# Seven block products for gate and up in all three feed-forwards, with the weight sums formed in DRAM

## The chip, the cores and the metric

The kernel runs on one core of a Trainium2 chip. The metric is the device time of one execution in microseconds (us). Before the change it is 2364.4 us, the median of three runs (2363.6 to 2364.85).

## The reference

Two transformer blocks follow each other, in float32, on 512 tokens of width 1024. The first block puts 16 meta tokens in front, so it works on 528. Cut to its frame:

```python
def first_block(...):                       # h: 528 tokens x 1024
    for l in range(2):
        hn = rmsnorm(h, norm_mix[l])
        h = h + (even_mixer if l == 0 else odd_mixer)(hn, ...)   # sparse attention + retention; stick-breaking attention
        h = h + conv_ffn(rmsnorm(h, norm_ffn[l]), ...)
    return rmsnorm(h, norm_final)[:, 16:528]

def conv_ffn(h, w_up, w_gate, conv_w, conv_b, w_down):           # 1024 -> 2816 -> 1024
    g = causal_conv3(h @ w_gate) + conv_b                        # over tokens, one filter per column
    return (silu(g) * (h @ w_up)) @ w_down

def second_block(x, ...):                                        # x: 512 tokens
    x = x + merge(four_mixers(rms_norm(x, attn_norm))) @ w_merge_out
    h = rms_norm(x, ffn_norm)
    return x + (silu(h @ w_gate) * (h @ w_up)) @ w_down
```

Each block ends its layers with a feed-forward: two `conv_ffn` in the first, one without a convolution in the second. The kernel calls them ffn0, ffn1 and ffn2.

## The kernel before

**Data.** The residual stream lies transposed in SBUF: eight tiles `h0` to `h7`, 128 columns of the model by 528 tokens. Weights lie in DRAM as tiles of 128 x 1024 float32 (512 KB): eight blocks of 128 x 128, one for each 128 rows of the contraction. A feed-forward has 22 tiles of hidden columns, f = 0 to 21, each with one weight tile for gate and one for up.

**A product.** `wtile` loads a weight tile into `w_raw` by a DMA on SP's queue, casts it to `w_hi` (float32r, on ScalarE or VectorE) and forms `w_lo` = `w_raw` - `w_hi` on VectorE. Each of the three names has three buffers. Activations come as the same kind of pair (`xh`, `xl`). `mm3` then makes three matmuls for each block: hi by hi, hi by lo, lo by hi. A plain projection of one weight tile over 528 tokens is two halves of 8 x 3 matmuls with 264 columns each; over 516 tokens they have 258, and over 512 tokens there are 24 matmuls of 512 columns.

**Order.** Every operation goes through the class `Order`, which only records. `flush`, once for each stage, is a list scheduler: it walks through modelled time with a cost for each operation (`cost`) and a delay between engines (`latency`), and issues on each engine the ready operation of lowest priority number. `O.shift -= 500` in `wtile` moves weight loads and their splits ahead by 500 operations. Some copies may go to ScalarE or VectorE, whichever is free first in the model. The chip then runs each engine's queue in that order. All recorded operations stand at one line of the file, L493.

**Stages.** The even mixer takes the span up to about 435 us, ffn0 to 806, the odd mixer to 1112, ffn1 to 1500, the second block's mixer to 1972, ffn2 to the end. Each stage ends with a prefetch of the next stage's first three weight tiles.

**ffn0 and ffn1 (`ffn`).** For each f, `gate_up` projects gate, scales it by the row norm `r`, convolves over tokens on VectorE (`y`), applies silu, projects up, multiplies, and splits the product into `ah`, `al`. Up works on 528 tokens in ffn0 and on 512 in ffn1. `down` takes hidden tiles in three groups, `GROUPS` (8, 8 and 6 tiles): all eight row blocks m of the output of a group come after the first tile of the next group, and `add_h` adds each onto `h`. The last group's row blocks are followed by `Following.add`, which prepares the next stage's `xh`, `xl` and the norm's sum of squares (`acc`).

**ffn2 (`block2_ffn`).** From f = 2 on (`FS`), gate and up are seen as a 2 x 2 block product (two halves of the contraction, two halves of the tokens) and made by `gate_up_fast` with seven half products instead of eight: 7 x 4 x 3 = 84 matmuls of 256 columns. The activations' sums `th`, `tl` are made once at the stage's start. The weights' sums `s13`, `s24` are made for each f in `weights`, on VectorE, by one addition of 1024 columns and two of 512 out of the loaded `r1`, `r2` (their names in the trace are `w_raw` and `s_raw`, since a `Ring` deals out the three `w_` places and two more `s_` places in turn).

**GpSimd** does nothing but its start-up; all DMAs are on SP's queue.

Of the kernel before, what the change touches and what calls it, by code (L numbers as in the profile page):

```python
# [11 lines left out]
F32 = mybir.dt.float32  # L12
# [16 lines left out]
GROUPS = ((0, 8), (8, 16), (16, 22))  # L29
# [160 lines left out]
def prepare(i):  # L190
# [23 lines left out]
    for n, (f0, f1) in enumerate(GROUPS):  # L214
        a[f"w_dn2_{n}"] = pack(i["w_down_2"][0][f0 * P:f1 * P], whole(0, D))
# [152 lines left out]
def latency(a, b):  # L368
    return 2.1 if a == "SP" else LAT.get((a, b), 0.25)
# [12 lines left out]
class Order:  # L382
# [30 lines left out]
    def cost(self, eng, method, out, ins, k):  # L413
# [19 lines left out]
        return 0.1 + n * 2.2e-3  # L433
# [151 lines left out]
def body(ctx: ExitStack, tc, A, out):  # L585
# [18 lines left out]
    class AllBanks:  # L604
# [35 lines left out]
    gg = cst.tile([P, KD], F32, name="gg")  # L640
    gcol = lambda n, k: gains[:, 8 * n + k:8 * n + k + 1]
# [12 lines left out]
    def wtile(name, i, kt=KD):  # L654
# [12 lines left out]
        O.shift += 500  # L667
        return v2(hi, P), v2(lo, P)
# [173 lines left out]
    def even_mixer():  # L842
        with ExitStack() as es:
            P_ = lambda name, **k: O.pool(es, name, **k)
            dr = P_("dr1", bufs=1, space=DRAM)
            ec = P_("ec", bufs=1)
# [268 lines left out]
            for m in range(RF, KD):  # L1115
                add(m)
            prefetch("w_gu0", 0, 1, 2)
            O.flush()

    def ffn(l, n):  # L1120
# [6 lines left out]
        with ExitStack() as es:  # L1127
# [8 lines left out]
            acts = {}  # L1136

            def gate_up(f):
                g = fp.tile([P, gw + 2], F32, name="g")
                V.memset(g[:, 0:2], 0.0)  # L1140
                proj(pall, wtile(f"w_gu{l}", 2 * f), x, times(g[:, 2:], r), grange)
                y = fp.tile([P, uw], F32, name="y", bufs=3)
# [6 lines left out]
                proj(pall, wtile(f"w_gu{l}", 2 * f + 1), xu, times(y, y), urange)  # L1149
                acts[f] = split_new(y, fp, "ah", "al", 10, uw)  # L1150

            def down(gi):
                f0, f1 = GROUPS[gi]
                a = [acts[f][0] for f in range(f0, f1)], [acts[f][1] for f in range(f0, f1)]
                if gi == 2:
                    if l == 0:
                        add = follow(lambda m: gcol(2, m), 0, fp, "y", 3)
                    else:
                        V.tensor_tensor(gg, gains[:, 32:40], gains[:, 40:48], op=ALU.mult)
                        add = follow(lambda m: gg[:, m:m + 1], NM, fp, "y", 3, lambda m: gcol(4, m))  # L1160
                for m in range(KD):
                    proj(pall, wtile(f"w_dn{l}_{gi}", m, f1 - f0), a, add_h(m, u0), urange)
                    if gi == 2:
# [11 lines left out]
    def odd_mixer():  # L1175
# [8 lines left out]
        with ExitStack() as es:  # L1184
            P_ = lambda name, **k: O.pool(es, name, **k)
            op = P_("op", bufs=1)
            x = nxt_[0].x
# [141 lines left out]
            out_proj(1, OSP, KD, follow(lambda m: gcol(3, m), Q0, op, "otmp", 2))  # L1329
            prefetch("w_gu1", 0, 1, 2)  # L1330
# [5 lines left out]
    def block2_mixer():  # L1336
        with ExitStack() as es:
# [5 lines left out]
            unit = lambda name, bufs=1, p=P, dt=F32: wk.tile([p, S], dt, name=name, bufs=bufs)  # L1343

# [377 lines left out]
            for m in range(KD):  # L1722
                proj(pall, wtile("w_mg", m), mgx, add_h(m, NM), ONE)
                add(m)
            prefetch("w_gu2", 0, 1, 2)
            O.flush()

    def block2_ffn():
        with ExitStack() as es:
# [6 lines left out]
            class Ring:  # L1736


                def __init__(self, dt, *places):
                    self.dt, self.places, self.n = dt, places, 0  # L1740

                def tile(self):
                    pl, name, bufs = self.places[self.n % len(self.places)]
                    self.n += 1
                    return pl.tile([P, D], self.dt, name=name, bufs=bufs)

            ring = lambda dt, a, b: Ring(dt, *((wp, a, 3), (fp, b, 2)) * 2, (wp, a, 3))
            raws, his, los = ring(F32, "w_raw", "s_raw"), ring(F32R, "w_hi", "s_hi"), ring(F32R, "w_lo", "s_lo")

            def early(fn):  # L1750
                O.shift -= 500
                v = fn()
                O.shift += 500
                return v

            def halves(raw, hi=None, lo=None):

                n = raw.shape[1]
                hi = his.tile()[:, :n] if hi is None else hi
                lo = los.tile()[:, :n] if lo is None else lo  # L1760
                SC.copy(hi, raw)
                V.tensor_tensor(lo, raw, hi.bitcast(F32), op=ALU.subtract)
                return v2(hi, P), v2(lo, P)

            def load(name, i, n=D):
                raw = raws.tile()[:, :n]
                dma(raw, A[name][i])
                return raw

            ts = []
            for k in range(KD // 2):
                g1, g2 = gcol(6, k), gcol(6, k + 4)
                h1, h2 = hT[k][:, NM:], hT[k + 4][:, NM:]
                tt = v2(raws.tile(), HS)
                th, tl = (fp.tile([P, 4, HS], F32R, name=f"{n}{k}", bufs=1) for n in ("th", "tl"))
                b22 = fp.tile([P, HS], F32, name="sp", bufs=2)
                SC.activation(b22, h2[:, HS:], AF.Copy, scale=g2)
                V.tensor_tensor(tt[:, 0, :], h1[:, :HS], h1[:, HS:], op=ALU.subtract)  # L1780
                SC.activation(tt[:, 0, :], tt[:, 0, :], AF.Copy, scale=g1)
                V.tensor_tensor(tt[:, 1, :], b22, tt[:, 0, :], op=ALU.add)
                V.scalar_tensor_tensor(tt[:, 2, :], h1[:, HS:], g1, b22, op0=ALU.mult, op1=ALU.subtract)
                V.scalar_tensor_tensor(tt[:, 3, :], h2[:, :HS], g2, tt[:, 1, :], op0=ALU.mult, op1=ALU.subtract)
                SC.copy(th, tt)
                V.tensor_tensor(tl, tt, th.bitcast(F32), op=ALU.subtract)
                ts.append((th, tl))
            tx = [[(h[:, j, :], l[:, j, :]) for h, l in ts] for j in range(4)]
            bx = lambda i, j: [(x[0][k][:, HS * j:HS * j + HS], x[1][k][:, HS * j:HS * j + HS]) for k in range(4 * i, 4 * i + 4)]

            def times3(ps, w, xs, first):
                wh, wl = w
                for k, (xh, xl) in enumerate(xs):
                    for i, (a, b) in enumerate(((wh, xh), (wh, xl), (wl, xh))):
                        T.matmul(ps, a[:, k, :], b, start=first and k == 0 and i == 0, stop=k == 3 and i == 2,
                                 skip_group_check=True)

            def bank():
                return pall.tile([P, 512], F32, name="d")

            def weights(f):


                r1, r2 = load("w_gs2", 2 * (f - FS)), load("w_gs2", 2 * (f - FS) + 1)
                s13, s24 = raws.tile(), raws.tile()
# [82 lines left out]
```

## Time and profile before

| | before |
|---|---|
| median of 3 runs | 2364.4 us (2363.6 to 2364.85) |
| the profiled execution | 2365.07 us |
| its span from first to last instruction | 2362.9 us |
| granted TensorE clock, mean | 0.998 of full speed |
| TensorE, VectorE, ScalarE, GpSimd busy | 99%, 76%, 41%, 0% |

The profiled execution is 2.2 us longer than its span, and 0.7 us longer than the median. In the rows below, PE is TensorE's matmuls, PEld its weight loads (they overlap), DVE is VectorE, ACT ScalarE, POOL GpSimd, and SPq SP's DMA queue. PEclk is the granted clock as a share of full speed. An "x" and a number count instructions; a released wait is written as the idle time before an instruction and what ended it.

### The profile page before, as it was taken

The numbers are of one execution on the slowest core, as the hardware profiler recorded it, in microseconds if no ns is written. First come the engines' busy times: TensorE is split into PE (matmuls) and PEld (weight loads), VectorE is DVE, ScalarE is ACT, GpSimd is POOL, SyncE is SP. The second block draws the span as 40 slices with busy tenths as digits, with TensorE's granted clock in tenths as the row PEclk, the third lists the DMA queues.
The fourth block names the chain that finished last, engine by engine and source line by source line (L and its number), as shares of the span: only waits on it lengthen the run. The fifth ranks groups of instructions, "written<-read, shape, count | busy, mean of one in ns | idle before, by whom it ended". The sixth has DMA issues, their size and how long they took to land.

```text
span 2362.9 us, 38568 instructions
## 1 busy us (share of the span) xinstructions
PE 2334.1 (99%) x15488; PEld 2125.5 (90%) x15488; DVE 1793.0 (76%) x3512; ACT 968.3 (41%) x1842; POOL 0.2 (0%) x4
## 2 busy tenths in 40 slices
PE   7999999999999999999999999999999999999999
PEld 7999999999999999999888888877888888889998
DVE  6999898764655779997665647876898877987965
ACT  4423556310111278885211203344677613443422
POOL 0000000000000000000000000000000000000000
PEclk9999999999999999999999999999999999999999
DMA  5222221322222211103223223322222122332322
GB/s 200 70 72 70 73 84 57 111 92 90 90 90 88 93 64 55 55 25 102 90 90 100 90 90 97 122 70 86 82 90 72 53 95 89 102 122 80 126 77 84
DMA packets 66546, 205.98 MB, mean 87 GB/s; under 512 B 7972, under 2 KB 14576, under 8 KB 66368
## 3 DMA queue, kind: packets, MB, share of 16 engines
q1 hardware_dynamic: 66368, 203.53, 27.1%
q8 instruction: 121, 1.98, 0.4%
q14 instruction: 57, 0.47, 0.1%
HBM read 201.37 MB, written 6.84 MB: 88 GB/s over the span
## 4 chain that ended last, share of the span: by engine, by line
PE 94%; DVE 3%; DMA 2%; issue 1%; ACT 1%; SPq 0%; DVEq 0%; ACTq 0%
PE d L493 54%; PE at L493 37%; PE pv L493 2%; DMA w_raw<-w_even 1%; DVE w_lo L493 1%; DVE s_lo L493 1%; DVE w_raw L493 0%; DMA w_raw<-w_gs 0%; DVE g L493 0%; DMA h<-h 0%; ACT w_hi L493 0%; DMA ob<-c_oh 0%; DVE sqh L493 0%; DVE s_raw L493 0%; SPq L493 0%
## 5 line engine op out<-in xcount | busy, mean ns | idle before, releaser
L493 PE MATMUL d<-xh,w_hi 128*128 128x264 f32 (+5 forms) x2082 | 616.2, 318 | 8.1 <-ACT w_hi L493 8.0
L493 PE MATMUL d<-xl,w_hi 128*128 128x264 f32 (+5 forms) x2082 | 618.4, 319 | 1.1 <-DVE xl L493 1.0
L493 PE MATMUL d<-xh,w_lo 128*128 128x264 f32 (+5 forms) x2082 | 614.0, 318 | 0.0
L493 DVE TENSOR_TENSOR w_lo<-w_raw,w_hi 128x1024 fp32r<-128x1024 f32 (+4 forms) x363 | 401.1, 1107 | 53.2 <-PE d L493 18.4
L493 PEld LDWEIGHTS d<-xh,w_hi 128*128 128x128 f32 x2082 | 377.4, 189 | 36.3 <-ACT w_hi L493 8.0
L493 PEld LDWEIGHTS d<-xl,w_hi 128*128 128x128 f32 x2082 | 377.3, 189 | 25.9 <-DVE xl L493 2.3
L493 PEld LDWEIGHTS d<-xh,w_lo 128*128 128x128 f32 x2082 | 376.3, 189 | 26.6 <-issue 1.9
L493 ACT CAST w_hi<-w_raw 128x1024 fp32r<-128x1024 f32 (+5 forms) x181 | 172.8, 955 | 328.2 <-PE d L493 230.5
L493 DVE CAST w_hi<-w_raw 128x1024 fp32r<-128x1024 f32 (+4 forms) x182 | 116.4, 640 | 188.0 <-PE d L493 113.0
L493 PE MATMUL at<-xh,w_hi 128*128 128x264 f32 (+3 forms) x822 | 240.1, 302 | 1.2 <-DVE h L493 1.2
L493 PE MATMUL at<-xh,w_lo 128*128 128x264 f32 (+3 forms) x822 | 240.1, 302 | 0.0
L493 PE MATMUL at<-xl,w_hi 128*128 128x264 f32 (+3 forms) x822 | 240.1, 302 | 0.0
L493 ACT ACTIVATE y<-g,cp 128x528 f32<-128x528 f32 (+1 forms) x44 | 36.2, 824 | 345.6 <-DVE g L493 345.6
L493 PEld LDWEIGHTS at<-xh,w_hi 128*128 128x128 f32 x822 | 152.8, 189 | 7.5 <-issue 1.6
L493 PEld LDWEIGHTS at<-xh,w_lo 128*128 128x128 f32 x822 | 152.8, 189 | 5.4
L493 PEld LDWEIGHTS at<-xl,w_hi 128*128 128x128 f32 x822 | 152.6, 189 | 5.2
L493 PE MATMUL at<-ah,w_lo 128*128 128x264 f32 (+1 forms) x350 | 113.0, 331 | 0.0
L493 PE MATMUL at<-ah,w_hi 128*128 128x264 f32 (+1 forms) x350 | 113.0, 332 | 0.0
L493 PE MATMUL at<-al,w_hi 128*128 128x264 f32 (+1 forms) x350 | 112.9, 332 | 0.0
L493 PE MATMUL d<-ah,w_hi 128*128 128x264 f32 (+1 forms) x274 | 91.1, 333 | 0.0
L493 PE MATMUL d<-al,w_hi 128*128 128x264 f32 (+1 forms) x274 | 91.0, 332 | 0.0
L493 PE MATMUL d<-ah,w_lo 128*128 128x264 f32 (+1 forms) x274 | 90.7, 332 | 0.0
(604 smaller groups left out, 4849.9 us busy)
## 6 DMA issues: line engine op xcount, KB each, us to landing
w_raw<-w_gu SPq DMA_DIRECT2D x92, 512.0 KB, 3.7
w_raw<-w SPq DMA_DIRECT2D x59, 512.0 KB, 3.6
w_raw<-w_dn SPq DMA_DIRECT2D x42, 512.0 KB, 3.8
w_raw<-w_even SPq DMA_DIRECT2D x41, 512.0 KB, 3.8
w_raw<-w_gs SPq DMA_DIRECT2D x25, 512.0 KB, 3.6
w_raw<-w_odd SPq DMA_DIRECT2D x24, 512.0 KB, 3.5
w_raw<-w_dn SPq DMA_DIRECT2D x21, 384.0 KB, 3.1
s_raw<-w_gs SPq DMA_DIRECT2D x15, 512.0 KB, 3.6
```

The costliest lines, as they stand in the source:

```text
L493: return f(*[r(x) for x in a], **{n: r(x) for n, x in k.items()})
```

## The change

**Block products everywhere.** The helpers of ffn2 move into a class `Fast`, used by all three feed-forwards. In ffn0 and ffn1 the tiles f = 2 to 21 now take `Fast.pair`: 84 matmuls of 264 columns (ffn0) or 258 (ffn1) in place of the plain projections. Up is then computed on all tokens before the silu and kept in `u`. The activations' sums are made at each stage's start, by eight tiles `t` taken from the weight ring. Where two token halves don't fit one 512-column PSUM bank, a fourth bank (`q2`) is taken, and `AllBanks` deals out eight banks, `pv` included.

**Weight sums in DRAM.** `add_blocks` replaces the three VectorE additions by five DMAs on GpSimd's queue, DRAM to DRAM: a copy and an accumulation for `s13`, a copy and two accumulations for `s24`. Four of the five write 512 KB and one 256 KB. With 20 tiles in three feed-forwards there are 300. Each set is issued during the mixer ahead of its feed-forward: `Ahead.plan` lists the 100 DMAs of a set, two tiles interleaved, and `Ahead.step`, called by `wtile`, copies one column of a fresh `w_hi` into a 32-column ring `ticks` (on ScalarE or VectorE), copies it on with GpSimd, and records the next two DMAs (three in the odd mixer). `Ahead.rest` records what is left at the mixer's end.

**Loads.** A fast tile then loads 1.75 MB by SP (`r1` 512 KB, half of `r2` 256 KB, `s13` and `s24` 512 KB each), where ffn0 and ffn1 loaded 1 MB and ffn2 loaded 1 MB.

**Down spread.** The groups are six (five in ffn2) of three to five tiles, and a group's eight row blocks are spread over the tiles of the next group. `ah`, `al` have 8 buffers in ffn0 and ffn1 (10 before), `y` two (three before). The planner's model gives a GpSimd operation 4.0 us and its results a latency of 2.1 us.

The core of the diff:

```diff
-GROUPS = ((0, 8), (8, 16), (16, 22))
+GROUPS = ((0, 4), (4, 8), (8, 12), (12, 16), (16, 19), (19, 22))
+GROUPS2 = ((0, 5), (5, 10), (10, 15), (15, 19), (19, 22))
...
-    return 2.1 if a == "SP" else LAT.get((a, b), 0.25)
+    return 2.1 if a in ("SP", "POOL") else LAT.get((a, b), 0.25)
...
-        return 0.1 + n * 2.2e-3
+        return 4.0
...
+            pl, place = ((pd, "d"), (pp, "at"), (pd, "d"), (pp, "at"), (pd, "d"), (pp, "at"), (pp, "at"), (pq, "pv"))[AllBanks.turn % 8]
...
+    far = pool("far", bufs=1, space=DRAM)
...
+    def add_blocks(name, i):
+        r1, r2 = A[name][2 * i], A[name][2 * i + 1]
+        two = lambda t: t.rearrange("p (a b) -> p a b", a=2)
+        twice_ = lambda r, c0: bass.AP(tensor=r.tensor, offset=r.offset + c0, ap=[[D, P], [0, 2], [1, 512]])
+        s13, s24 = (far.tile([P, D], F32, name=f"{name}{n}{i}") for n in ("a", "b"))
+        block_sums[name, i] = s13, s24
+        return [lambda: G.dma_start(two(s13), twice_(r2, 0)),
+                lambda: G.dma_start(s13, r1, accum_op=ALU.add, max_dma_last_dim=4 * D),
+                lambda: G.dma_start(two(s24), s13[:, None, :512].to_broadcast([P, 2, 512])),
+                lambda: G.dma_start(two(s24), twice_(r1, 512), accum_op=ALU.add),
+                lambda: G.dma_start(s24[:, 512:], r2[:, 512:], accum_op=ALU.add)]
...
+        def plan(name, rate):
+            every = [add_blocks(name, i) for i in range(NFT - FS)]
+            Ahead.todo = [op for a in range(0, len(every), 2) for both in zip(*every[a:a + 2]) for op in both]
...
+        def step(seen):
+            Ahead.seen += 1
+            if Ahead.todo and Ahead.seen > 6:
+                n, Ahead.n = Ahead.n % 32, Ahead.n + 1
+                O.copy(ticks[:, n:n + 1], seen)
+                G.tensor_copy(ticks[:, 32 + n:33 + n], ticks[:, n:n + 1])
+                for op in Ahead.todo[:Ahead.rate]:
+                    op()
...
+        Ahead.step(hi[:, 0:1].bitcast(F32))
...
+            Ahead.plan("w_gs0", 2)
...
+            Ahead.rest()
             prefetch("w_gu0", 0, 1, 2)
...
+    class Fast:
...
+            for k in range(KD // 2):
...
+                b22 = fp.tile([P, w], F32, name="sp", bufs=2)
+                SC.activation(b22, h22, AF.Copy, scale=g2)
+                t = [v2(self.raws.tile()[:, :2 * w], w) for _ in range(2)]
+                V.tensor_tensor(t[0][:, 0, :], h11, h12, op=ALU.subtract)
...
+                V.scalar_tensor_tensor(t[1][:, 1, :], h21, g2, t[0][:, 1, :], op0=ALU.mult, op1=ALU.subtract)
+                for i in range(2):
+                    h, l = (fp.tile([P, 2, w], F32R, name=f"{n}{i}{k}", bufs=1) for n in ("th", "tl"))
+                    SC.copy(h, t[i])
+                    V.tensor_tensor(l, t[i], h.bitcast(F32), op=ALU.subtract)
...
+        def blocks(self, f):
+            i = f - FS
+            r1, r2 = self.load(A[self.name][2 * i]), self.load(A[self.name][2 * i + 1][:, 512:])
+            s13, s24 = (self.load(t) for t in block_sums[self.name, i])
+            w1, w24, w13 = self.halves(r1), self.halves(s24), self.halves(s13)
...
     def ffn(l, n):
...
+            fast = Fast(fp, f"w_gs{l}", lambda k: gcol(n, k), g0, hw, 1)
...
+                if f < FS:
+                    proj(pall, wtile(f"w_gu{l}", 2 * f), x, times(g[:, 2:], r), grange)
+                else:
+                    u = fp.tile([P, gw], F32, name="u", bufs=1)
+                    fast.pair(f, g[:, 2:], u, r)
-                y = fp.tile([P, uw], F32, name="y", bufs=3)
+                y = fp.tile([P, uw], F32, name="y", bufs=2)
...
-                acts[f] = split_new(y, fp, "ah", "al", 10, uw)
+                    V.tensor_tensor(y, u[:, o:], y, op=ALU.mult)
+                acts[f] = split_new(y, fp, "ah", "al", 8, uw)
...
-                    if gi and f == f0:
-                        down(gi - 1)
-            down(2)
+                    if gi:
+                        down(gi - 1, range(KD * (f - f0) // (f1 - f0), KD * (f + 1 - f0) // (f1 - f0)))
+            down(len(GROUPS) - 1, range(KD))
...
     def block2_ffn():
...
-                V.tensor_tensor(two(s13), two(r2)[:, 0:1, :].to_broadcast([P, 2, 512]), two(r1), op=ALU.add)
-                V.tensor_tensor(s24[:, :512], s13[:, :512], r1[:, 512:], op=ALU.add)
-                V.tensor_tensor(s24[:, 512:], s24[:, :512], r2[:, 512:], op=ALU.add)
```

GpSimd's queue before, in full (its start-up):

```order
L1881 ISA
L1881 MEMSET const-float32-0.0 128x1
L1881 MEMSET const-float32-1.0 128x1
L1881 MEMSET const-bfloat16-1.0 128x1
L1881 MEMSET const-uint8-127 128x1
L1884 UNCONDITIONAL_BRANCH x2
L1884 ISA
```

The same queue after, at the place of the first paced DMAs in the even mixer (`w_gs0a` and `w_gs0b` are the DRAM tiles `s13` and `s24`; a copy of `ticks` is the pacing instruction):

```order
L495 DMA w_gs0b_0_1630<-w_gs 256x1x512
L495 DMA w_gs0b_0_1686<-w_gs 256x1x512
L495 DMA w_gs0a_0_2296<-w_gs 256x1x512
L495 DMA w_gs0a_0_2356<-w_gs 256x1x512
L495 COPY ticks_572<-ticks_572 128x1 x12
L495 DMA w_gs0b_0_1198<-w_gs 128x512
L495 DMA w_gs0b_0_1256<-w_gs 128x512
L495 DMA w_gs0b_0_1314<-w_gs 128x512
L495 COPY ticks_572<-ticks_572 128x1
```

38 more DMAs stand ahead of these rows: the planner puts 42 DMAs ahead of the first twelve `ticks` copies.

SP's queue in ffn0 before, around the first group's down (`w_gu` gate and up tiles, `w_dn` down tiles):

```order
L493 DMA w_raw_6408<-w_gu 128x1024
L493 DMA w_raw_6472<-w_gu 128x1024
L493 DMA w_raw_6536<-w_dn_0 128x1024
L493 DMA w_raw_6606<-w_dn_0 128x1024
L493 DMA w_raw_6664<-w_dn_0 128x1024
L493 DMA w_raw_6732<-w_dn_0 128x1024
L493 DMA w_raw_6792<-w_dn_0 128x1024
L493 DMA w_raw_6861<-w_dn_0 128x1024
L493 DMA w_raw_6917<-w_dn_0 128x1024
L493 DMA w_raw_6975<-w_dn_0 128x1024
L493 DMA w_raw_7033<-w_gu 128x1024
```

The same queue after, at two fast tiles in the second half of ffn0 (`w_gs` is `r1` or half of `r2`):

```order
L495 DMA w_raw_7698<-w_dn_1 128x512
L495 DMA w_raw_7711<-w_gs0a_0_519 128x1024
L495 DMA s_raw_7744<-w_gs0b_0_1686 128x1024
L495 DMA w_raw_7802<-w_dn_1 128x512
L495 DMA w_raw_7859<-w_gs 128x512
L495 DMA w_raw_7877<-w_gs 128x1024
L495 DMA s_raw_7902<-w_dn_1 128x512
L495 DMA s_raw_7915<-w_gs0a_0_2296 128x1024
L495 DMA w_raw_7948<-w_gs0b_0_4763 128x1024
```

The eight loads of a group's down in a row have become loads of half the size (a group has four tiles of 128 rows), one to three between the loads of fast tiles.

VectorE in ffn2 before, between two fast tiles (`w_raw`, `s_raw` as outputs are the weight sums):

```order
L493 TENSOR_TENSOR g_0_22818<-g_0_22818,rrow_21788 128x512
L493 TENSOR_TENSOR g_0_22818<-u_0_22821,g_0_22818 128x512
L493 TENSOR_TENSOR w_raw_22908<-s_raw_22802,w_raw_22882 128x1024
L493 TENSOR_TENSOR al_22921<-g_0_22818,ah_22911 128x512
L493 TENSOR_TENSOR w_lo_22925<-s_raw_22763,w_hi_22916 128x1024
L493 TENSOR_TENSOR h_0_119<-at_22875,h_0_119 128x512
L493 TENSOR_TENSOR s_raw_22936<-w_raw_22908,w_raw_22882 128x512
L493 TENSOR_TENSOR s_raw_22936<-s_raw_22936,s_raw_22802 128x512
L493 TENSOR_TENSOR h_0_123<-d_22914,h_0_123 128x512
```

VectorE after, at about the same place:

```order
L495 TENSOR_TENSOR w_lo_25394<-s_raw_25254,w_hi_25381 128x1024
L495 TENSOR_TENSOR sv_25333<-at_25330,sv_25333 128x256
L495 TENSOR_TENSOR s_lo_25410<-w_raw_25204,s_hi_25399 128x1024
L495 TENSOR_TENSOR g_0_25378<-sv_25333,rrow_23919 128x256
L495 TENSOR_TENSOR h_0_101<-at_25397,h_0_101 128x512
L495 TENSOR_TENSOR g_0_25378<-g_0_25378,rrow_23919 128x512
L495 TENSOR_TENSOR w_lo_25443<-s_raw_25317,w_hi_25428 128x640
L495 TENSOR_TENSOR g_0_25378<-u_0_25350,g_0_25378 128x512
L495 CAST ah_25466<-g_0_25378 128x512
```

The three additions are gone, and splits of down tiles with 640 columns (`w_lo` from a group of five) stand between the operations of the fast tile.

## Rows read from the trace of the kernel before

**Rows 1.** The page: the span, and each engine busy (share, instructions).

```profile
span 2362.9 us, 38568 instructions
...
PE 2334.1 (99%) x15488; PEld 2125.5 (90%) x15488; DVE 1793.0 (76%) x3512; ACT 968.3 (41%) x1842; POOL 0.2 (0%) x4
```

**Rows 2.** Busy times by stretch, columns in the first line: three stages.

```profile
core 0: us, PE busy (x) PEld busy (x) DVE busy (x) ACT busy (x) POOL busy (x), PEclk, DMA share, GB/s
60.00:435.00 375.00, 374.66 (x2923) 361.17 (x2922) 341.63 (x900) 177.32 (x377) 0.00 (x0) 1.00 0.24 74
...
480.00:780.00 300.00, 300.00 (x2458) 300.00 (x2457) 180.13 (x287) 46.29 (x58) 0.00 (x0) 1.00 0.28 89
...
1112.00:1500.00 388.00, 387.26 (x2201) 339.12 (x2201) 248.06 (x377) 79.56 (x109) 0.00 (x0) 1.00 0.30 95
```

**Rows 3.** The same view, short stretches of one matmul width (512, 258, then 256).

```profile
1214.20:1261.40 47.20, 47.20 (x208) 38.70 (x207) 23.55 (x31) 2.51 (x3) 0.00 (x0) 1.00 0.27 90
1397.25:1402.05 4.80, 4.80 (x41) 4.76 (x40) 3.21 (x4) 0.00 (x0) 0.00 (x0) 1.00 0.57 159
2024.70:2098.50 73.80, 68.76 (x565) 67.31 (x564) 70.35 (x111) 32.36 (x43) 0.00 (x0) 1.00 0.37 120
2145.80:2221.80 76.00, 73.28 (x601) 72.78 (x600) 67.72 (x106) 32.25 (x43) 0.00 (x0) 0.98 0.30 98
2275.00:2322.70 47.70, 47.26 (x396) 47.00 (x395) 41.17 (x65) 20.60 (x28) 0.00 (x0) 1.00 0.32 99
```

**Rows 4.** VectorE's groups by shape, 480 to 800 us: columns in the first line.

```profile
line engine op names shapes xcount | busy us, mean ns | idle before us <-releasers
L493 DVE TENSOR_TENSOR w_lo<-w_raw,w_hi 128x1024 fp32r<-128x1024 f32 x51 | 62.2, 1220 | 3.1 <-PE at L493 1.7 <-PE d L493 0.6
L493 DVE SCALAR_TENSOR_TENSOR y<-g,cp,y 128x528 f32<-128x528 f32 x38 | 29.1, 766 | 0.7
...
L493 DVE TENSOR_TENSOR al<-y,ah 128x528 fp32r<-128x528 f32 x19 | 13.4, 703 | 0.1
...
L493 DVE TENSOR_TENSOR g<-at,rrow 128x264 f32<-128x264 f32 x21 | 9.0, 430 | 13.8 <-PE at L493 13.8
```

**Rows 5.** The same view, 1985 to 2330 us: 512-column halves, block adds.

```profile
L493 DVE TENSOR_TENSOR s_lo<-w_raw,s_hi 128x512 fp32r<-128x512 f32 x13 | 8.9, 686 | 0.0
L493 DVE TENSOR_TENSOR w_raw<-s_raw,w_raw 128x1024 f32<-128x1024 f32 x7 | 8.5, 1218 | 0.7 <-DMA w_raw<-w_gs 0.7
```

**Rows 6.** The same view, 1440 to 1520 us: what follows each row block of down.

```profile
L493 DVE SCALAR_TENSOR_TENSOR xl<-h,gg,xh 128x512 fp32r<-128x512 f32 x8 | 5.7, 746 | 0.0
...
L493 DVE TENSOR_TENSOR acc<-acc,y 128x512 f32<-128x512 f32 x7 | 4.8, 687 | 0.3
```

**Rows 7.** Busy times by stretch, columns as in rows 2: the first microseconds.

```profile
5.00:10.00 5.00, 2.03 (x7) 1.73 (x8) 2.57 (x4) 3.14 (x5) 0.00 (x0) 1.00 1.00 366
...
50.00:55.00 5.00, 3.81 (x17) 3.55 (x18) 3.35 (x7) 3.75 (x9) 0.00 (x0) 0.60 0.00 1
```

**Rows 8.** The chain that ended last, in its first 50 us: start, length, what.

```profile
4.00 6.23 DMA h<-h
10.25 4.83 DMA ob<-c_oh
...
30.43 19.03 DMA w_raw<-w_even
```

**Rows 9.** TensorE in order of time: start, length, what, idle before.

```profile
51.19 0.58 PE L493 MATMUL at<-ikh,iqsa 128*128 128x256 f32 x1 [4.82 <-ACT ikh L493]
```

**Rows 10.** DMA issues: transfer, queue, count, KB each, median us to landing.

```profile
w_raw<-w_gu SPq DMA_DIRECT2D x92, 512.0 KB, 3.7
...
bv<-bv SPq DMA_DIRECT2D x1, 3068.0 KB
```

**Rows 11.** ScalarE in order of time: the 39th cast of a weight tile.

```profile
298.22 0.84 ACT L493 CAST w_hi<-w_raw 128x768 fp32r<-128x768 f32 x1 [1.21 <-PE d L493]
```

**Rows 12.** VectorE's groups, 60 to 435 us: casts of weight tiles.

```profile
L493 DVE CAST w_hi<-w_raw 128x1024 fp32r<-128x1024 f32 (+1 forms) x14 | 9.1, 651 | 4.5 <-PE d L493 4.5
```

More of the change, by code (lines that the diff above doesn't have):

```diff
@@ L640, in body @@
     gg = cst.tile([P, KD], F32, name="gg")
+    ticks = cst.tile([P, 64], F32, name="ticks")
     gcol = lambda n, k: gains[:, 8 * n + k:8 * n + k + 1]
@@ L1116, in even_mixer, with __init__, tile, early @@
                 add(m)
+            Ahead.rest()
             prefetch("w_gu0", 0, 1, 2)
             O.flush()
+    class Ring:
+        def __init__(self, dt, *places):
+            self.dt, self.places, self.n = dt, places, 0
+        def tile(self):
+            pl, name, bufs = self.places[self.n % len(self.places)]
+            self.n += 1
+            return pl.tile([P, D], self.dt, name=name, bufs=bufs)
+    def early(fn):
+        O.shift -= 500
+        v = fn()
+        O.shift += 500
+        return v
@@ L1329, in odd_mixer @@
             out_proj(1, OSP, KD, follow(lambda m: gcol(3, m), Q0, op, "otmp", 2))
+            Ahead.rest()
             prefetch("w_gu1", 0, 1, 2)
@@ L1724, in block2_mixer @@
                 add(m)
+            Ahead.rest()
             prefetch("w_gu2", 0, 1, 2)
@@ L1734, in block2_ffn @@
             acts = {}
[L1736 to L1796, printed above, removed]
@@ L1838, in gate_up_fast, with gate_up @@
+            fast = Fast(fp, "w_gs2", lambda k: gcol(6, k), NM, HS, 2)
+            def gate_up(f):
+                g = fp.tile([P, S], F32, name="g2", bufs=2)
+                if f < FS:
+                    proj(pall, wtile("w_gu2", 2 * f), x, times(g, r), ONE)
+                else:
+                    u = fp.tile([P, S], F32, name="u2", bufs=2)
+                    fast.pair(f, g, u, r)
                 SC.activation(g, g, AF.Silu)
                 V.tensor_tensor(g, g, r, op=ALU.mult)
-                V.tensor_tensor(g, u, g, op=ALU.mult)
+                if f < FS:
+                    proj(pall, wtile("w_gu2", 2 * f + 1), x, times(g, g), ONE)
+                else:
+                    V.tensor_tensor(g, u, g, op=ALU.mult)
@@ L1853, in down @@
-            def down(gi):
-                f0, f1 = GROUPS[gi]
-                n = (f1 - f0) * P
+            def down(gi, ms):
+                f0, f1 = GROUPS2[gi]
                 a = [acts[f][0] for f in range(f0, f1)], [acts[f][1] for f in range(f0, f1)]
-                for m in range(KD):
-                    w = early(lambda: halves(load(f"w_dn2_{gi}", m, n)))
+                for m in ms:
+                    w = early(lambda: fast.halves(fast.load(A[f"w_dn2_{gi}"][m])))
                     proj(pall, w, a, add_h(m, NM), ONE)
-                    if gi == 2:
+                    if gi == len(GROUPS2) - 1:
@@ L1861, in down @@
                         dma(out[P * m:P * m + P, :], hT[m][:, NM:])
-            for gi, (f0, f1) in enumerate(GROUPS):
+            for gi, (f0, f1) in enumerate(GROUPS2):
                 for f in range(f0, f1):
                     gate_up(f)
-                    if gi and f == f0:
-                        down(gi - 1)
-            down(2)
+                    if gi:
+                        down(gi - 1, range(KD * (f - f0) // (f1 - f0), KD * (f + 1 - f0) // (f1 - f0)))
+            down(len(GROUPS2) - 1, range(KD))
```

141 lines of the change are left out of this document (88 added, 53 removed).

## The prediction

> **What bounds the kernel now.** I read the page first. TensorE's matmuls fill 99% of the span; VectorE is busy 76% and GpSimd not at all [rows 1]. So time can go only by fewer matmul columns or by TensorE's idle stretches, and I read the stages next, from the table of busy times by stretch. In the plain feed-forward ffn0 TensorE has no gap at all in 300 us, while VectorE is 60% busy; ffn1 has next to none [rows 2]. The even mixer is as full on TensorE, and VectorE there is 91% busy. Then short stretches of one matmul width give the pitch of a matmul, the stretch divided by the gaps between starts (count less one) [rows 3]: 264 columns 300.00/2457 = 0.1221 us [rows 2]; 258 columns 4.80/40 = 0.120; 512 columns 47.20/207 = 0.228; 256 columns, in ffn2, 47.70/395 = 0.1208 where VectorE is 86% busy, but 73.80/564 = 0.1309 where it is 95% and 76.00/600 = 0.1267 where it is 89%. ffn2 thus loses time to VectorE. The first 50 us are a chain of loads [rows 8].
>
> **What goes.** ffn0: a fast tile has 84 matmuls of 264 columns instead of 96; 20 tiles x 12 x 0.1221 = 29.3 us. ffn1: gate had 48 of 258 columns and up 24 of 512, and the tile now has 84 of 258, so 480 x 0.228 - 720 x 0.120 = 109.4 - 86.4 = 23.0 us. ffn2 keeps its matmuls, but three additions of 1.218 + 2 x 0.686 = 2.6 us [rows 5] leave VectorE in each of 20 tiles, and down's row blocks no longer come in a lump; I take both stalls as gone: 564 x (0.1309 - 0.1208) + 600 x (0.1267 - 0.1208) = 5.7 + 3.5 = 9.2 us. Late next there is TensorE itself. Together 61.5 us.
>
> **What comes, with both ends.**
> VectorE in ffn0 and ffn1, steady. For a fast tile with two row blocks of down I count three splits of 1024 columns, three of 512 (half of `r2`, two of down), two convolution steps, three operations of 528 columns and eleven of 264: 3 x 1.220 + 3 x 0.686 + 2 x 0.766 + 3 x 0.703 + 11 x 0.430 = 14.1 us [rows 4, 5], against 132 matmuls x 0.1221 = 16.1 us: 87%. In ffn1 it is about 13.7 against 15.6. Forty such tiles are 634 us of TensorE. At that load the trace shows no loss in one place (86% in ffn2, and 91% in the even mixer, where TensorE has 374.66 of 375 us) and 4.7% in another (89%): 0 to 30 us. I take 1.5%, 9 us, nearer to the 86% row.
> The sums of activations. Four steps of two additions, two fused operations, and two splits of 528: 4 x (4 x 0.430 + 2 x 0.703) = 12.5 us of VectorE, wanted before the first fast tile. Cover is two plain tiles, 2 x 96 x 0.1221 = 23.4 us, in which VectorE already has 60%, 14 us [rows 2]: 26.5 against 23.4, so 3 us late, and the same in ffn1. 6 us; 0 if the prefetched splits or the first fast tiles (no down yet) absorb it, 10 if not.
> The last group. It now has three tiles, so a row block of down is 9 x 0.228 = 2.1 us of TensorE in ffn1, against some 3.4 us of VectorE: a split of 384 columns (estimate 0.55, between 0.430 and 0.686), the addition onto `h` 0.686, `xl` 0.746 and two sums of 0.687 [rows 6]. With six tiles it was 4.1 us and hid this. Eight row blocks are 10 us late in ffn1, and by 2.2 against 2.9 some 6 in ffn0: up to 16 us; but splits run ahead in the five weight places and the next stage waited for its norm before too, so 4 us.
> The start. GpSimd's DMAs are free to go from the first microsecond: 42 stand ahead of the first pacing copy. There the DMA engines are full at 366 GB/s [rows 7], and the chain waits 6.23 + 4.83 us for loads and 19.03 us for a weight tile queued behind the 3068 KB DRAM-to-DRAM `bv` [rows 8, 10], 30.1 us in all. TensorE's wait for `ikh` at 51.19 us, at a granted clock of 0.60 after it, follows from that chain and would move with it [rows 7, 9]. No GpSimd DMA is in the trace. Its price is bounded below by `bv`, 3068 KB in 19.0 us or 3.2 us for 512 KB, and above by three passes of a 512 KB load, 3 x 3.7 = 11 us [rows 8, 10], since an accumulation reads twice and writes. I take 4 us, nearer to the row that is DRAM to DRAM. That is 131 GB/s, 36% of 366. The chain's 30.1 us grows by 0 to 30 us; I take 9, somewhat under 36% as not all of it is transfer.
> By the Trainium skill (DMA: Bandwidth & Descriptors, section Queues, rings and completion order) each DMA engine goes round the queues that have work, packet by packet. That would give SP about half, and 30 us here instead of 9; no row shows two busy queues.
> Loads in ffn0 and ffn1. A fast tile with its down wants 2.25 MB in 16.1 us, 140 GB/s, where the stage moved 89 [rows 2]; with GpSimd's next sets behind it (33 DMAs of the second run on in ffn0) 271 of 366. The nearest wait is 0.7 us for seven tiles' loads in ffn2 [rows 5], 4 us for 40. I take 4; 0 to 40 us, if each tile waits 1 us.
> Nothing for the pacing copies: 134 of one column, 118 of them on ScalarE, busy 41%. Nothing for the place of a set: at 4 us its 100 DMAs take 400 us, before ffn0 begins.
> Sum of costs 9 + 6 + 4 + 9 + 4 = 32 us. The profiled execution is 2365.1 us: 2365.1 - 61.5 + 32 = 2335.6, and 0.7 less for the median, 2335 us.
>
> **Rivals.**
> VectorE is the new bound in ffn0 and ffn1. For it: the 95% row, 7.7% lost (0.1208 against 0.1309); against it: 86% without loss. At 7.7% of 634 us the cost is 49 instead of 9, and the time 2375, slower by 10.
> Transfers take the gain: start 30 instead of 9 and loads 40 instead of 4, up to 2392, the middle 2363. For it the full DMA engines at 5 us; against it a DMA share of 0.24 to 0.30 in the stages [rows 2].
> The pacing ring stalls ScalarE, slower. `ticks` has 32 columns, so the 33rd copy waits until GpSimd has read the first, and that stands behind 42 DMAs. The 33rd goes with the 39th tile, cast at 298.22 us in the even mixer [rows 11]. From 298/42 = 7.1 us for a DMA this decides; below it costs nothing. Behind the copy on ScalarE wait the casts to `w_hi`, for which TensorE waits. At 11 us GpSimd comes to its copy at 462 us: +164, 2499 us.
> GpSimd holds VectorE up. In the even mixer VectorE has 9% of slack [rows 2], and its casts of 1024 columns take 651 ns, half of a subtraction's 1220 [rows 4, 12]; if each of these 14 and of some 30 scalings beside them waited 2 us for GpSimd, 44 x 2 = 88 us less some cover is 81, and the time 2416. If it waited 1 us, the slack of 33 us would leave some 11.
> The Trainium skill (SBUF — State Buffer, section Who interferes with whom) says that such VectorE operations, in a mode with two ports, and GpSimd lock each other out of a shared pair. Of this no row shows anything, since GpSimd is idle before.
>
> **How the numbers follow.** Forecast 0.62: its own range 2303 (no cost at all) to 2353. VectorE as bound 0.12, transfers 0.10, the ring 0.08, the port 0.08. A difference of 0.2%, about 5 us, is what a measurement can tell from none. Faster: the forecast whole, 0.62, and about 0.09 from the lower parts of the first two rivals; same 0.06 from their middles; slower 0.23, the rest. The range 2302 to 2382 takes in the forecast, VectorE as bound, and most of the transfers: about 0.8.
>
> **What would show it.** Each step has its row after: ffn0 from first to last fast tile at 16.1 us a tile; matmuls of 258 columns at 0.120 in ffn1; 256 columns at 0.121 throughout ffn2, VectorE under 87%. The chain of the first 50 us about 9 us longer. GpSimd's DMAs at about 4 us from one to the next, the first set done near 400 us. Against it: waits of TensorE for `w_lo` or `s_lo` in ffn0 (VectorE), for loads of `w_gs` (transfers), ScalarE waiting for GpSimd near 300 us (ring), VectorE's casts in the even mixer far above 651 ns (port). What makes it wrong first is the price of a GpSimd DMA, which nothing before shows.

## The result and the profile after

The changed kernel takes 2464.2 us (median of 4 runs, 2461.3 to 2464.6) against 2364.6 us: 1.0419 of before, 95% interval 1.0401 to 1.0437. It is 100 us slower; 2335 was forecast. Its page, in the lines of [rows 1], with two queue lines below (packets, MB, time of its packets as a share of 16 engines' span):

```profile
span 2462.1 us, 40793 instructions
...
PE 2323.3 (94%) x15488; PEld 2122.4 (86%) x15488; DVE 1898.8 (77%) x3840; ACT 1181.0 (48%) x2267; POOL 305.8 (12%) x438
...
q1 hardware_dynamic: 92864, 250.73, 31.1%
q0 software_dynamic: 50880, 141.58, 26.4%
```

TensorE's busy time fell by only 11 us, at a mean granted clock of 0.973 where it was 0.998, and it is now idle for 139 us where it was idle for 29. Where, the busy times by stretch tell, columns as in [rows 2]; first two rows of before, then the changed kernel:

```profile
0.00:50.00 50.00, 37.34 (x261) 33.93 (x261) 29.79 (x54) 21.76 (x35) 0.20 (x4) 1.00 0.69 234
50.00:130.00 80.00, 78.74 (x574) 75.67 (x575) 73.11 (x162) 34.82 (x70) 0.00 (x0) 0.96 0.20 62
```

```profile
0.00:50.00 50.00, 24.59 (x91) 19.21 (x91) 16.27 (x31) 17.18 (x25) 17.38 (x27) 0.94 1.00 295
50.00:130.00 80.00, 32.97 (x224) 32.13 (x225) 22.18 (x37) 10.84 (x25) 17.09 (x21) 0.67 0.93 240
535.00:625.00 90.00, 77.19 (x575) 74.90 (x574) 61.28 (x108) 36.95 (x50) 20.83 (x25) 0.94 1.03 286
650.00:850.00 200.00, 200.00 (x1645) 200.00 (x1644) 162.60 (x285) 88.41 (x123) 0.00 (x0) 1.00 0.47 145
1205.00:1360.00 155.00, 135.87 (x902) 124.22 (x902) 112.53 (x198) 67.27 (x98) 39.14 (x47) 0.96 1.00 280
2150.00:2450.00 300.00, 300.00 (x2064) 278.36 (x2063) 220.88 (x357) 110.81 (x150) 0.00 (x0) 1.00 0.45 144
```

In the first 130 us TensorE has 315 matmuls, where before it has 835; then in the first half of ffn0 and of ffn1 it waits again. In all three places the DMA share is 0.93 to 1.03 and GpSimd is at work: the trace has 42 of its DMAs in a row from 1.3 us, 35 of the second set from 506 us and 49 of the third from 1200 us, each time ahead of the first pacing copy of their set. Where GpSimd is done (650 to 850 us, and 2150 to 2450 us in ffn2), TensorE has no gap. The start in the chain that ended last, against [rows 8]:

```profile
3.07 12.14 DMA h<-h
15.23 20.09 DMA c_id<-c_id
35.39 23.61 DMA w_raw<-w_even
...
75.70 43.71 another core or an unknown queue
```

The waits are the same kind of loads as before, but 30.1 us have become 99.6 (12.14 + 20.09 + 23.61 + 43.71). For the last, 43.71 us, the chain names no releaser, but ScalarE's own row at its end does:

```profile
119.51 1.04 ACT L495 CAST w_hi<-w_raw 128x1024 fp32r<-128x1024 f32 x1 [43.81 <-DMA w_raw<-w_even]
```

It is the seventh cast of a weight tile, the same at which the last row of [rows 8] ends, where the wait was 19.03 us. The transfers of 5 to 50 us, first before (SP's queue alone), then after; columns are packets, MB, and share of the engines' time:

```profile
q1 hardware_dynamic: 4147, 10.80, 69.3%
```

```profile
q0 software_dynamic: 2412, 8.79, 72.1%
q1 hardware_dynamic: 2386, 5.08, 31.9%
```

GpSimd's queue (q0) has 72% of the engines' time (the two shares add up to more than 100%, since the times of packets can overlap), and SP moves 5.08 MB where it moved 10.80.

### The profile page after: what moved, and what is told of

It reads as the page before. It is cut to its first block, busy times and chain, and to the rows that moved or that the text cites. A ratio compares the mean times of both kernels' runs of the same rounds, so it can differ in the third digit from the quotient of the medians.

```text
span 2462.1 us, 40793 instructions
## 1 busy us (share of the span) xinstructions
PE 2323.3 (94%) x15488; PEld 2122.4 (86%) x15488; DVE 1898.8 (77%) x3840; ACT 1181.0 (48%) x2267; POOL 305.8 (12%) x438
## 4 chain that ended last, share of the span: by engine, by line
PE 80%; DMA 9%; DVE 5%; ACT 3%; another core or an unknown queue 2%; issue 1%; SPq 0%; ACTq 0%; DVEq 0%
PE d L495 45%; PE at L495 28%; PE pv L495 7%; DMA s_raw<-w_dn 1%; DMA bt<-bv 1%; DVE w_lo L495 1%; DMA w_raw<-w_even 1%; DMA w_raw<-w_gs1a 1%; DMA c_id<-c_id 1%; DMA w_raw<-w_gu 1%; DMA w_raw<-w_gs 1%; ACT w_hi L495 1%; DMA h<-h 0%; DVE s_lo L495 0%
## 5 line engine op out<-in xcount | busy, mean ns | idle before, releaser
L495 PE MATMUL d<-xh,w_hi 128*128 128x264 f32 (+4 forms) x1616 | 495.3, 331 | 37.2 <-ACT w_hi L495 12.0
L495 PE MATMUL d<-xl,w_hi 128*128 128x264 f32 (+4 forms) x1616 | 496.8, 330 | 0.0
L495 PE MATMUL d<-xh,w_lo 128*128 128x264 f32 (+5 forms) x1616 | 487.3, 328 | 0.0
L495 DVE TENSOR_TENSOR w_lo<-w_raw,w_hi 128x1024 fp32r<-128x1024 f32 (+5 forms) x322 | 320.9, 998 | 80.3 <-ACT w_hi L495 67.4
L495 ACT CAST s_hi<-w_raw 128x512 fp32r<-128x512 f32 (+3 forms) x112 | 89.8, 811 | 110.6 <-PE at L495 55.8
L495 DVE TENSOR_TENSOR s_lo<-w_raw,s_hi 128x512 fp32r<-128x512 f32 (+3 forms) x112 | 102.9, 927 | 25.2 <-ACT s_hi L495 22.1
L495 PE MATMUL at<-xh,s_hi 128*128 128x264 f32 (+2 forms) x356 | 101.4, 285 | 1.2 <-ACT s_hi L495 0.8
L495 PE MATMUL at<-xh,s_lo 128*128 128x264 f32 (+2 forms) x356 | 101.5, 285 | 0.1
L495 PE MATMUL at<-xl,s_hi 128*128 128x264 f32 (+2 forms) x356 | 101.4, 285 | 0.0
L495 PE MATMUL d<-th,s_hi 128*128 128x264 f32 (+2 forms) x284 | 82.2, 289 | 10.9 <-ACT s_hi L495 6.3
L495 DVE TENSOR_TENSOR s_lo<-s_raw,s_hi 128x1024 fp32r<-128x1024 f32 (+3 forms) x74 | 72.1, 976 | 13.0 <-ACT s_hi L495 12.1
```

Source lines behind the costliest of these rows:

```text
L495: return f(*[r(x) for x in a], **{n: r(x) for n, x in k.items()})
```

## The experiments

The verdicts stand against runs of the kernel before on the same chip (2365.0 to 2365.6 us). Lines of diffs are cut to the edit.

**The 42 DMAs alone, added to the kernel before.**

```diff
+        for i in range(tiles):                       # tiles = 10, extra = 2
+            G.dma_start(two(a[i]), twice_(r[i][1], 0))
+        for i in range(tiles):
+            G.dma_start(a[i], r[i][0], accum_op=ALU.add, max_dma_last_dim=4 * D)
...
+            flood("w_gs2", 10, 2)
```

> The kernel before with one thing added: 42 DMAs on GpSimd's queue from DRAM to DRAM, of the sizes and in the order of those ahead of the first pacing copy, whose results nobody reads. No pacing copies, no block products. Theory (transfers at the start): 2364 + 69 = 2433, within 2415 to 2445, all of it in the first 130 us. Rival (the loss at the start comes from anything else in the change): 2364 to 2372.

Measured 2437.6 us, 1.0305 (1.0290 to 1.0321): +72 us. The stretches of the start repeat those of the changed kernel:

```profile
0.00:50.00 50.00, 23.23 (x91) 18.63 (x91) 16.10 (x31) 17.00 (x25) 17.39 (x27) 0.90 1.00 293
50.00:130.00 80.00, 28.17 (x189) 27.33 (x189) 17.92 (x31) 9.49 (x20) 16.53 (x19) 0.65 0.95 236
```

The 300th matmul starts at 133.5 us instead of 58.8, and hardly anything is lost after that. These DMAs alone, without any other part of the change, make the loss at the start.

**The same 42 DMAs with an eighth of the bytes.**

```diff
-            G.dma_start(a[i], r[i][0], accum_op=ALU.add, max_dma_last_dim=4 * D)
+            G.dma_start(a[i][:16], r[i][0][:16], accum_op=ALU.add, max_dma_last_dim=4 * D)
```

> The kernel before with the same 42 unread GpSimd DMAs at the start, in the same order, but each on 16 of the 128 rows, so an eighth of the bytes. Theory (the loads of the start lose their share of the DMA engines to GpSimd's bytes): an eighth of 72 us, 2370 to 2380. Rival (the number of DMAs on the second queue, or GpSimd's work in issuing them, is what costs, whatever they move): most of the 72 us stays, above 2400.

Measured 2368.7 us, 1.0015 (1.0006 to 1.0024): +3.7 us, a little under the theory's range. GpSimd issued all 42 in the first 50 us and was busy with it for 28.08 us, against 33.9 us in the first 130 of the run above, but TensorE hardly waits:

```profile
0.00:50.00 50.00, 39.40 (x261) 35.96 (x261) 29.95 (x54) 21.34 (x34) 28.08 (x46) 1.00 0.84 271
50.00:130.00 80.00, 73.52 (x546) 70.67 (x547) 69.10 (x155) 34.12 (x67) 0.00 (x0) 0.94 0.22 71
```

It is what the DMAs move, not their number nor GpSimd's work. Bytes and packets went down together here, so this run doesn't tell which of the two counts.

**The DMAs really paced.**

```diff
-                G.tensor_copy(ticks[:, 32 + n:33 + n], ticks[:, n:n + 1])
+                c = G.tensor_copy(ticks[:, 32 + n:33 + n], ticks[:, n:n + 1])
                 for op in Ahead.todo[:Ahead.rate]:
-                    op()
+                    o = op()
+                    c.succ.append(o)
+                    o.need += 1
```

> The changed kernel, with each GpSimd DMA made to follow its pacing copy in the planner too, so that none is issued ahead of the seventh weight tile. Theory (transfers: the 42 DMAs ahead of the first pacing copy fill the DMA engines and hold the first loads up, 69 us in the first 130): the first 300 matmuls are again done near 60 us instead of 128, and the time falls by 50 to 75 us from 2464, to 2390 to 2415, not more, since the same 300 DMAs still run, some beside ffn0 and ffn1. Rival (the pacing copies on ScalarE and VectorE, or GpSimd and VectorE locking each other out, are what costs): the copies and the DMAs are all still there, so 2450 to 2475.

Measured 2391.7 us, 1.0111 (1.0091 to 1.0131): 73 us better than the change, as the theory has it. The start is that of before again (300th matmul at 59.3 us), with GpSimd idle in the first 50 us:

```profile
0.00:50.00 50.00, 38.85 (x261) 35.71 (x261) 29.88 (x54) 21.53 (x35) 0.20 (x4) 1.00 0.69 233
50.00:130.00 80.00, 78.15 (x566) 74.67 (x567) 72.26 (x161) 34.81 (x77) 10.57 (x18) 0.96 0.47 126
...
1110.00:1160.00 50.00, 39.68 (x243) 35.32 (x243) 35.96 (x68) 27.67 (x43) 13.97 (x16) 0.91 1.07 267
```

Still 26 us slower than before. The last row shows one place: at ffn1's start the second set still runs, the DMA share is 1.07, and TensorE loses 10 of 50 us.

**No sums at all, and the copies alone.**

```diff
-        Ahead.step(hi[:, 0:1].bitcast(F32))
...
-            s13, s24 = (self.load(t) for t in block_sums[self.name, i])
+            s13, s24 = (self.load(A[self.name][2 * i + n]) for n in (1, 0))
```

> The changed kernel without any GpSimd DMA or pacing copy; the two sums that SP loads are replaced by two weight tiles of the same size, so the weight sums are left out of the computation and only its time counts. Theory (transfers): everything lost goes, the first 130 us (69), the stretch to 500 us (16), the starts of ffn0 (20) and ffn1 (29), so 2464 - 134 = 2330, within 2315 to 2345. Rival (VectorE is the new bound in the feed-forwards, or the spread down and the short last groups cost): above 2360, with TensorE waiting for VectorE inside ffn0 and ffn1.

Measured 2318.0 us, 0.9794 (0.9779 to 0.9809), in the theory's range. So the block products and the spread down are worth 47.6 us, net of all that they cost on TensorE and VectorE. From the paced kernel only the DMAs were then taken out:

```diff
-                for op in Ahead.todo[:Ahead.rate]:
-                    o = op()
```

> The paced kernel with its 134 pacing copies on ScalarE or VectorE and their 134 copies on GpSimd, but without the 300 DMAs; SP loads weight tiles of the same size in place of the sums, so the sums are left out. It stands between the kernel without sums (2318) and the paced one (2392). Theory (transfers alone): the copies cost nothing, 2316 to 2324. Rival (the copies hold ScalarE in its order, waits of up to 10.6 us in the trace): most of the 74 us stays, above 2340, above all in the odd mixer (8 us) and the second block's mixer (17 us), where ScalarE waits before such copies.

Measured 2341.3 us, 0.9899 (0.9884 to 0.9914): neither theory, since 23 of the 74 us are far from nothing, and not most. With the copies in, the kernel is 23 us slower, and the paced DMAs make the other 50. Set against this run, TensorE in the paced kernel is 13.5 us late at the start of the odd mixer and 39.5 us late at the end of ffn1, so most of the 50 us is lost in ffn1. How the copies cost 23 us is shown in part only. ScalarE waits in front of them (what waited, total us, times, longest):

```profile
ACT ticks L495 <- DVE w_hi L495: 58.7, 22, 10.2
```

Where VectorE casts the tile, the copy on ScalarE stands in ScalarE's queue until that cast comes, and what is behind it waits too. But the longest waits of TensorE that the kernel without sums doesn't have (4.36 us at 252 us, 2.15 and 4.17 us at 1788 and 1795 us) don't stand behind such a wait: the planner, with the copies in its list, lays out another order on all engines. How the 23 us divide between copies and order stays open.

**Sums on VectorE.**

```diff
+            s13, s24 = self.raws.tile(), self.raws.tile()
+            V.tensor_tensor(two(s13), two(r2)[:, 0:1, :].to_broadcast([P, 2, 512]), two(r1), op=ALU.add)
+            V.tensor_tensor(s24[:, :512], s13[:, :512], r1[:, 512:], op=ALU.add)
+            V.tensor_tensor(s24[:, 512:], s24[:, :512], r2[:, 512:], op=ALU.add)
```

> The changed kernel with the weight sums made by three VectorE additions in each fast tile of all three feed-forwards, as ffn2 had them; no GpSimd DMA. VectorE then has 14.1 + 2.6 = 16.7 us of work in a fast tile of ffn0 against 16.1 us of matmuls. Theory (transfers): 2330 as without sums, plus 0.6 us and some stalls of the 8 per cent kind in 40 tiles, plus the 9 us of ffn2: 2350 to 2400, far under 2464. Rival (VectorE load is what decides): close to or above 2400, with ffn0 and ffn1 longer than before.

Measured 2336.8 us, 0.9876 (0.9860 to 0.9893), faster than before and under the range that I expected. In steady ffn0 VectorE is 93% busy and TensorE has no gap; at the start of ffn0, where VectorE also makes the activations' sums, TensorE loses 5.8 of 60 us:

```profile
520.00:780.00 260.00, 260.00 (x2135) 260.00 (x2134) 240.86 (x426) 115.41 (x160) 0.00 (x0) 1.00 0.31 95
...
460.00:520.00 60.00, 54.24 (x425) 52.14 (x424) 56.30 (x95) 28.29 (x39) 0.00 (x0) 1.00 0.31 100
```

So VectorE's load isn't free: this kernel is 18.8 us slower than the one without sums, and loses where the work comes in a burst.

**Down spread alone, in ffn2 of the kernel before.**

```diff
-                    if gi and f == f0:
-                        down(gi - 1)
+                    if gi:
+                        down(gi - 1, range(KD * (f - f0) // (f1 - f0), KD * (f + 1 - f0) // (f1 - f0)))
```

> The kernel before with one part of the change alone: in ffn2, down in five groups with the row blocks spread over the next group's tiles. The sums stay on VectorE, no block products in ffn0 and ffn1. Theory (the stalls of ffn2 came from the eight row blocks in a lump, not from VectorE's share): ffn2 gains the 12.8 us that it gained with VectorE's sums, 2351 to 2355. Rival (the three additions are what filled VectorE, as the prediction had it): 0 to 4 us gained, 2361 to 2366.

Measured 2354.1 us, 0.9951 (0.9936 to 0.9966): 11 us, as the theory has it, 9.4 of them in ffn2 (353.2 to 343.8 us from its norm row to the end). In the changed kernel ffn2 takes 338.1 us. So the lump of row blocks made most of ffn2's stalls. With down spread and the additions left on VectorE, in the kernel with sums on VectorE above, it takes 340.4 us: the additions are worth some 2 us of the 15, and what makes the rest isn't shown.

**Sums on GpSimd in SBUF.**

```diff
-            V.tensor_tensor(two(s13), two(r2)[:, 0:1, :].to_broadcast([P, 2, 512]), two(r1), op=ALU.add)
+            G.tensor_tensor(two(s13), two(r2)[:, 0:1, :].to_broadcast([P, 2, 512]), two(r1), op=ALU.add)
```

> The same sums by three additions in SBUF on GpSimd instead of VectorE or DMAs, in all 60 fast tiles. Theory (VectorE and transfers both free): VectorE at 83 per cent as in the kernel without sums, no more transfers than with VectorE's sums: 2316 to 2330. Rival (GpSimd's additions are slow or hold VectorE up): TensorE waits for the splits of the sums, above 2345; the length of a VectorE operation beside them shows it.

In this run the planner's model also has its cost and latency for GpSimd of the kernel before. Measured 2428.5 us, 1.0278 (1.0258 to 1.0298). The rival holds, in its second half: GpSimd's additions hold VectorE up. VectorE's groups by shape, 480 to 800 us, with the sums on VectorE, then on GpSimd:

```profile
L495 DVE SCALAR_TENSOR_TENSOR y<-g,cp,y 128x528 f32<-128x528 f32 x40 | 30.5, 762 | 0.1
```

```profile
L495 DVE SCALAR_TENSOR_TENSOR y<-g,cp,y 128x528 f32<-128x528 f32 x36 | 59.6, 1655 | 1.9 <-ACT y L495 1.5
```

The same operation takes 1655 ns on the mean instead of 762. The trace tells when: 5 of the 36 don't overlap an addition of GpSimd and take 759 ns, the 31 that do take 1800.

**DMAs for four tiles, VectorE for sixteen.**

```diff
-            every = [add_blocks(name, i) for i in range(NFT - FS)]
+            every = [add_blocks(name, i) for i in range(NS)]          # NS = 4
...
-            Ahead.plan("w_gs0", 2)
+            Ahead.plan("w_gs0", 1)
```

> Weight sums by GpSimd's DMAs for the first four fast tiles of each feed-forward only (60 DMAs in all, one for each pacing copy), by VectorE for the other 16. Theory: with VectorE's sums (2337) TensorE lost 16 us at the starts of the feed-forwards, where VectorE also makes the activations' sums, and nothing later, with VectorE 93 per cent busy; DMAs for these tiles take that away and are few enough not to disturb the loads: 2318 to 2328. Rival (any GpSimd DMA disturbs the loads in proportion: 74 us for 300, so 15 for 60): 2335 to 2345.

Measured 2323.9 us, 0.9823 (0.9808 to 0.9837), in the theory's range. The start of ffn0 is nearly whole again:

```profile
460.00:520.00 60.00, 59.02 (x484) 58.81 (x483) 53.04 (x93) 28.07 (x40) 0.00 (x0) 1.00 0.42 131
```

**A longer last group, and half the copies.**

```diff
-GROUPS = ((0, 4), (4, 8), (8, 12), (12, 16), (16, 19), (19, 22))
+GROUPS = ((0, 4), (4, 8), (8, 11), (11, 14), (14, 18), (18, 22))
```

> The kernel with GpSimd's sums for four tiles (2324), and the six groups of ffn0 and ffn1 cut so that the last has four tiles instead of three (4, 4, 3, 3, 4, 4). Theory (at the stage's end VectorE's 3.4 us a row block outlasts the 2.1 us of matmuls, which is the 6.3 us stall seen at the end of ffn1 in each kernel with short groups): 2.7 us of matmuls against 3.5, so 8 x 0.5 = 4 us gained in ffn1, less in ffn0, 2317 to 2321. Rival (the stall is the next stage waiting for its norm, whatever the group): 2322 to 2326.

Measured 2315.7 us, 0.9800 (0.9783 to 0.9816), 8.2 us better where the theory had 4. TensorE at the end of ffn1, with three tiles and with four:

```profile
1453.07 1.44 PE L496 MATMUL at<-qsa,rb 32*8 32x383 f32 x2 [6.15 <-DVE h L496]
```

```profile
1447.85 1.03 PE L496 MATMUL at<-qsa,rb 32*8 32x383 f32 x2 [2.90 <-DVE h L496]
```

Before, this matmul had no wait. At ffn0's end three waits of 1.00, 1.20 and 1.09 us are gone too. Then the copies were halved:

```diff
-            Ahead.plan("w_gs0", 1)
+            Ahead.plan("w_gs0", 2)
```

> The kernel with the last group of four, with two DMAs for each pacing copy instead of one: 30 copies instead of 60. Theory (134 copies cost 23 us, so 60 some 10 and 30 some 5): 4 to 6 us below the kernel with 60 copies. Rival (with few DMAs the copies are hidden): within 2 us of it.

Measured 2313.2 us, 0.9787 (0.9771 to 0.9803), 2.6 us better, between theory and rival; by their ranges the two can't be told apart. It is the fastest kernel here, 52 us under the kernel before.

## Why the prediction was wrong

The steps, each as the difference of two kernels that were run:

| term | forecast | measured | from |
|---|---|---|---|
| block products and spread, less VectorE's load, activations' sums, last groups | -42.5 | -47.6 | before to no sums |
| pacing copies, with the order that the planner makes of them | 0 | +23 | no sums to copies alone |
| DMAs, each behind its pacing copy | 4 (0 to 40) | +50 | copies alone to paced |
| DMAs ahead of their pacing copies | 9 (0 to 30) | +73 | paced to the change |

**The step that failed is the start**, put at 9 us. The 300th matmul comes at 128.1 us in the changed kernel and at 59.3 in the paced one: 69 of the last row's 73 us. What is left of that row lies behind the start: there the bursts of 35 and 49 DMAs in ffn0 and ffn1 stand against what the same DMAs cost elsewhere when paced. The price of a GpSimd DMA was about right: the 42nd landed at 138.0 us, 3.3 us each, near the lower bound. The share was not. I made it 36%, the DMAs' 131 GB/s of 366, as though GpSimd took its part of the bytes and left the rest to SP. With work on both queues it took 72% of the engines' time. The sum had a slip besides: if 36% of the engines are taken, a load on what is left takes 1/0.64 = 1.56 times as long, so even my own share makes 17 us of 30.1, not 9. And the 30.1 us of chain were no frame for the loss: the DMA share is 0.98 to 1.07 from 10 to 110 us and the last of the 42 DMAs lands at 138, so each load that the longer chain brought into that time was late too. The seventh weight tile is one of them, and the 23.61 us before it are a wait that the chain of before doesn't have. So the upper end of 30 us, from one queue in two, was no bound. The clock adds to it: with TensorE waiting, the granted clock over 50 to 130 us was 0.67 on the mean against 0.96 before, and 0.50, the lower level (1.2 GHz), from 90 to 120 us, in which TensorE had no matmul.

**Loads beside later sets** were priced by 0.7 us of waiting in ffn2, a stage in which nothing else used the engines. At 535 to 625 us the chain waits 7.8 to 9.9 us for each of six loads of 256 and 512 KB; one of 512 KB lands in 3.7 us where nothing is beside it [rows 10]. The rival "transfers take the gain" had the mechanism, but took its price (at most 2392) from the same two steps.

**The copies** were put at nothing by ScalarE's 41%. A share says nothing of an instruction that waits at the head of its queue for another engine, nor of what the planner does to the order to make room for it.

**What held, in part by luck.** Matmuls removed and their pitch held. The first row's 47.6 us for 42.5 is a near hit of terms that are each off. ffn2's gain, forecast 9.2 from two stretches of 150 us together, was 15.1 (353.2 to 338.1 us), with down's lump as its main cause. VectorE's load cost nothing in the steady tiles (9 forecast): it came to 81% there (162.60 of 200 us), not 87%, and the 95% row, taken for a limit, was a burst. The activations' sums cost nothing either (6 forecast): without weight sums TensorE has no wait above 0.3 us in ffn0 and ffn1 ahead of their last groups. The last group cost more than the 4 us that I took of its 16. In the changed kernel TensorE stands idle 3.4 us at the end of ffn0 and 8.7 at the end of ffn1, and the granted clock falls with it, where before it has no gap (one of the two waits at ffn1's end, 2.6 us, is still there with a last group of four, so what makes it isn't shown). ffn1's end after, then before:

```profile
1578.00:1612.00 34.00, 25.27 (x100) 19.20 (x101) 22.02 (x38) 13.46 (x24) 2.85 (x4) 0.83 0.41 114
```

```profile
1495.00:1530.00 35.00, 35.00 (x156) 27.84 (x155) 25.24 (x39) 7.90 (x11) 0.00 (x0) 1.00 0.43 136
```

**The other rivals.** GpSimd reached its first pacing copy at 120.84 us, long before 298: no ring stall. The first set was done at 514 us, not near 400, since its last 58 DMAs did wait for copies. VectorE's casts in the even mixer, the row of [rows 12] from 130 to 505 us after, are as long as before:

```profile
L495 DVE CAST w_hi<-w_raw 128x1024 fp32r<-128x1024 f32 (+1 forms) x12 | 7.7, 645 | 3.4 <-PE d L495 3.4
```

None of the casts of 1024 columns in this row overlaps an issuing of a DMA by GpSimd, so the row alone tests little. Over the whole trace 66 subtractions of 1024 columns do, and take 1218 ns (1221 the others); so do eight casts of 1024 columns, of 742 ns on the mean (691 the others), two of them 818 and 978. So GpSimd's DMAs held VectorE up by very little.

## What to carry to other kernels

A list scheduler lets a DMA with nothing to wait for go at once, wherever the program records it (the first at 1.3 us here); a program's order is no pacing unless the DMA depends on the pacing instruction. Price background transfers by the time for which they hold the DMA engines while critical loads run, not by their bytes against a peak. And look at how evenly an engine's work comes before its busy share is called a limit: 93% cost nothing here in steady tiles, and the same work cost TensorE 5.8 of 60 us where it came in a burst.

## What the runs showed of the hardware

Two busy queues didn't share the engines' time evenly. From 5 to 50 us GpSimd's queue had 2412 packets and SP's 2386, from 535 to 625 us 4505 and 4494; but GpSimd's took 72.1% and 61.8% of the time, SP's 31.9% and 40.6%, so that a packet of GpSimd's DRAM-to-DRAM DMAs held an engine 2.2 and 1.5 times as long as one of SP's. At the start its packets were also larger (8.79 MB against 5.08); for each MB they held the engines 1.3 times as long, and in ffn0 1.6 times. The Trainium skill (DMA: Bandwidth & Descriptors, section Queues, rings and completion order) has each engine go round the queues that have work, packet by packet. The counts of these two stretches agree with it; those of 70 to 100 us (1986 and 856, with `bv` under way on SP's queue) don't by themselves, and no row shows whether SP had work on every engine there. The half that the prediction drew from it held neither for time nor, at the start, for bytes.

GpSimd's additions in SBUF lengthened most VectorE operations beside them that read both inputs from SBUF. From 480 to 800 us the fused operation above took 759 ns alone and 1800 where it overlapped an addition; the addition onto `h`, with one input from PSUM, took 422 ns alone and 423 where it overlapped (21 of 34). The Trainium skill (SBUF — State Buffer, section Who interferes with whom) has VectorE's operations with two SBUF inputs contend with GpSimd's reads, which agrees. The subtractions of 1024 columns into `w_lo` and `s_lo` kept their 1220 ns because all but two of 55 met no addition; of the two, one took 1226 ns and one 3405.
